# An expert stage's gated products: their transposes and parts one unit of weights sooner, their activation ahead of the context's second products

## The chip, the core and the metric

The kernel runs on one core of one Trainium2 chip. The metric is device time in microseconds (us) of one execution, lower is better. Five engines work side by side, each through its own queue in order: TensorE (PE in the profile, with PEld for the loading of its weights), VectorE (DVE), ScalarE (ACT), GpSimd (POOL) and SyncE (SP, which here only issues loads).

## The reference, cut to what matters

The network has two layers. Each ends in an expert stage: 16 experts of 1024 x 512 gate and up weights and 512 x 1024 down weights, in float32. Each expert takes the `cap` tokens that score highest for it: 128 of the 1024 latent tokens, and in the first layer also 32 of the 256 context tokens.

```python
def expert_choice_ffn(h, w_router, w_gate, w_up, w_down):
    n, dm = h.shape[1], h.shape[2]
    cap = EC_FACTOR * n // N_EXPERTS
    aff = jax.nn.softmax(jnp.einsum('bnd,de->bne', h, w_router).astype(jnp.float32), axis=-1)
    g, idx = lax.top_k(aff.swapaxes(1, 2), cap)
    xs = jax.vmap(lambda hb, ib: hb[ib])(h, idx)
    act = jax.nn.silu(jnp.einsum('becd,edf->becf', xs, w_gate)) * jnp.einsum('becd,edf->becf', xs, w_up)
    ys = jnp.einsum('becf,efd->becd', act, w_down) * g[..., None].astype(h.dtype)
    ...
for l in range(DEPTH):
    need_ctx = l < DEPTH - 1
    ...
    x = x + mod_l[5] * expert_choice_ffn(h, moe_router[l], moe_w_gate[l], moe_w_up[l], moe_w_down[l])
    if need_ctx:
        ...
        ctx = ctx + mod_c[5] * expert_choice_ffn(hc, moe_router[l], moe_w_gate[l], moe_w_up[l], moe_w_down[l])
```

## The kernel before

Almost every operation is recorded at line 162, a helper, so the rows are told apart by tiles: `A` holds the rounded weights and their remainders (and the context's tokens), `C` the raw weights as loaded, `W` the tokens' parts and the results, `M` small tiles, among them the gated products, and `ps` the PSUM banks.

**One unit of weights** is 512 KB: 256 rows of a gate or an up matrix, or 128 rows of a down matrix. An expert has twelve: four pairs of gate and up, four of down. `sources` gives their order of loading, in which expert e-1's down units come between the first and the second half of expert e's gate and up units. `fetch` loads a unit into one of ten `C` buffers, on SP's queue. `issue` splits it: ScalarE copies it rounded into `hi` (`A<-C`, ACTIVATE), VectorE subtracts to `lo` (`A<-C,A`, TENSOR_TENSOR). In layer 1 every sixth subtraction goes to GpSimd instead. Three products, high by high, low by high and high by low, stand for one in full precision.

**One expert** in `experts`, under a manual schedule, in which each engine keeps the order in which the code emits: four calls of `gate_up` (k = 0 to 3, each six 128x512 products of one unit, then the `issue` of a later unit), in layer 0 the context's products with the same four raw units (`ctx`, 64 products `ps<-C,A`, after which the four `C` buffers are free and four loads are issued), then `down` for expert e-1 (four units, 24 products `ps<-A,M`, in layer 0 followed by 32 products `ps<-C,M` of the context), then the next tokens' parts (`parts`), four more `gate_up` calls (k = 4 to 7), `ctx` for these units, and `activate`. In layer 1 (`need` is false) there is no context work, and `issue` itself fetches the next unit.

**Around the change.** `activate` makes the gated product `act`: ScalarE's Silu of the gate's bank (`M<-ps`, 128x512 f32), then VectorE's product with the up bank (`M<-M,ps`); in layer 0 also a 128x128 one for the context. One expert later `turn(e-1)`, called after `gate_up` of k = 1, transposes `act` on TensorE (four `ps<-cf,M`, and in layer 0 a fifth for the context), copies the result rounded to `ah` on ScalarE (`M<-ps`, fp32r) and subtracts to `al` on VectorE (`M<-ps,M`). In layer 0 ScalarE also copies the context's part. `down` needs `ah` for its first two products and `al` from its third on. In three experts (e = 1, 5, 9) `slots` makes the next routing table: VectorE builds tiles after k = 0, TensorE takes them in eight products `ps<-M,M` after k = 3.

The last expert's `turn` and `down` (e = 16) run after the loop's weights are through.

Of the kernel before, what the change touches and what calls it, by code (L numbers as in the profile page):

```python
# [15 lines left out]
AF = mybir.ActivationFunctionType  # L16
# [25 lines left out]
         g=7, v=0.079, hgrn0=6.614, hgrn1=6.757, group0=1.91, group1=3.41, hout0=6.767, hout1=3.44, chunk=6.713, prep=1.5,  # L42
# [123 lines left out]
class Model:  # L166
# [1651 lines left out]
    def experts(self, l, need, base, basec, h2d, h2c):  # L1818
# [4 lines left out]
        nc, a = self.nc, self.a  # L1823
# [4 lines left out]
        X, XT, XC, ACT, AT = {}, {}, {}, {}, {}  # L1828
# [14 lines left out]
        def fetch(gone=0):  # L1843
            nonlocal live
            live -= gone
            while live < raws:
                s = next(src, None)
                if s is None:
                    return
                w = self.t("C", [128, D])  # L1850
                nc.sync.dma_start(w, s)
                raw.append(w)
                live += 1

        def issue(early=False):
            nonlocal unit
            if not raw:
                return
            w = raw.pop(0)
            u = unit % ring  # L1860
            hi, lo = rows[u], rows[ring + u]
            nc.scalar.activation(hi, w, AF.Copy)
            (nc.gpsimd if early or (not need and unit % 6 == 5) else nc.vector).tensor_sub(lo, w, hi.bitcast(F32))
            unit += 1
            ready.append((w, hi, lo))
            if not need:
                fetch(1)

        def prep(e):
            it, vt = self.it[:, e:e + 1], self.vt[:, e:e + 1]  # L1870
            X[e] = (self.gather(h2d, it), it, vt)
# [28 lines left out]
                nc.vector.tensor_sub(xl[:, hs], pt, xh[:, hs].bitcast(F32))  # L1900
            return xh, xl

        def gate_up(e, u, g, p):

            xh, xl = XT[e]
            w, hi, lo = ready.pop(0)
            for k in range(2):
                c = slice(512 * k, 512 * k + 512)
                for pas, (xx, ww) in enumerate(((xh, hi), (xl, hi), (xh, lo))):
                    nc.tensor.matmul(p, xx[:, 2 * u + k], ww[:, c], start=(u == 0 and k == 0 and pas == 0),  # L1910
                                     stop=(u == 3 and k == 1 and pas == 2))
            issue()
            return u, g, w

# [8 lines left out]
                                         stop=(u == 3 and k == 1 and g == 1))  # L1923
                fetch(1)

        def activate(e, pg, pu, pc):
            act = self.t("M", [128, 512])
            nc.scalar.activation(act, pg, AF.Silu)
            nc.vector.tensor_mul(act, act, pu)
            actc = None  # L1930
            if need:
                actc = self.t("M", [128, 128])
                nc.scalar.activation(actc, pc[:, 0:128], AF.Silu)
                nc.vector.tensor_mul(actc, actc, pc[:, 128:256])
            ACT[e] = (act, actc)

        def turn(e):

            act, actc = ACT.pop(e)
            pt = self.p([128, 4, 128])  # L1940
            for i in range(4):
                nc.tensor.transpose(pt[:, i, :], act[:, 128 * i:128 * i + 128], self.ident)
            ah = self.t("M", [128, 4, 128], F32R)
            al = self.t("M", [128, 4, 128], F32R)
            nc.scalar.activation(ah, pt, AF.Copy)
            nc.vector.tensor_sub(al, pt, ah.bitcast(F32))
            ct = None
            if need:
                pt = self.p([128, 4, 128])
                nc.tensor.transpose(pt[:, 0, :], actc, self.ident)  # L1950
                ct = self.t("M", [128, 128])
                nc.scalar.activation(ct, pt[:, 0, :], AF.Copy)
            AT[e] = (ah, al, ct)

        def down(e):
            _, it, vt = X.pop(e)
            ah, al, ct = AT.pop(e)
            py = [self.p() for _ in range(2)]
            units = []
            for f in range(4):  # L1960
                w, hi, lo = ready.pop(0)
                for pas, (xx, ww) in enumerate(((ah, hi), (al, hi), (ah, lo))):
                    for hf in range(2):
                        nc.tensor.matmul(py[hf], xx[:, f], ww[:, 512 * hf:512 * hf + 512],
                                         start=(f == 0 and pas == 0), stop=(f == 3 and pas == 2))
                issue()
                units.append(w)
                yield "s"
            if need:
                pyc = self.p()  # L1970
                for f, w in enumerate(units):
                    for q in range(4):
                        nc.tensor.matmul(pyc[32 * q:32 * q + 32, :256], ct[:, 32 * f:32 * f + 32],
                                         w[:, 256 * q:256 * q + 256], start=f == 0, stop=f == 3)
                    fetch(1)
            ys = self.t("W", [128, D])
            for hf in range(2):
                c = slice(512 * hf, 512 * hf + 512)
                nc.vector.scalar_tensor_tensor(ys[:, c], py[hf], vt, G5[hf], op0=ALU.mult, op1=ALU.mult)
            nc.gpsimd.indirect_dma_start(out=base, out_offset=bass.IndirectOffsetOnAxis(ap=it, axis=0),  # L1980
                                         in_=ys, in_offset=None, compute_op=ALU.add)
            if need:
                yc = self.t("M", [128, 256])
                nc.vector.scalar_tensor_tensor(yc, pyc[:, :256], self.vc[:, e:e + 1], G5c, op0=ALU.mult, op1=ALU.mult)
                nc.gpsimd.indirect_dma_start(out=basec.rearrange("n (q d) -> (n q) d", q=4),
                                             out_offset=bass.IndirectOffsetOnAxis(ap=self.ic4[:, e:e + 1], axis=0),
                                             in_=yc, in_offset=None, compute_op=ALU.add)
# [20 lines left out]
        with self.tc.manual_schedule():  # L2008
            prep(0)
            yield True  # L2010
            prep(1)
            issue()
            yield 3.0
            XT[0] = parts(X[0][0])
            while len(ready) < ahead:
                issue()
            for e in range(17):
                if e < 16:
                    pg, pu = self.p(), self.p()
                    pc = self.p() if need else None  # L2020
                    units = []
                    for k in range(4):
                        units.append(gate_up(e, k // 2, k % 2, (pg, pu)[k % 2]))
                        if k == 1 and e:
                            turn(e - 1)
                        if e % 4 == 1 and e < 12:
                            if k == 0:
                                table = self.slots(e // 4 + 1)
                            if k in (0, 3):
                                next(table)  # L2030
                        if k == 0 and e + 2 < 16:
                            prep(e + 2)
                        yield "s"
                    if need:
                        ctx(e, units, pc)
                        yield "s"
                else:
                    turn(e - 1)
                if e:
                    yield from down(e - 1)  # L2040
                    yield "s"
                if e < 16:
                    if e % 4 == 1 and e < 12:
                        next(table, None)
                    if e + 1 < 16:
                        if need and (e + 1) % 4 == 0:
                            turn_ctx((e + 1) // 4)
                        XT[e + 1] = parts(X[e + 1][0])
                        if need and e % 4 == 1 and e < 12:
                            gather_ctx(e // 4 + 1)  # L2050
                    units = []
                    for k in range(4, 8):
                        units.append(gate_up(e, k // 2, k % 2, (pg, pu)[k % 2]))
                        yield "s"
                    if need:
                        ctx(e, units, pc)
                    activate(e, pg, pu, pc)
                yield "s"

    def layer(self, l):  # L2060
# [83 lines left out]
```

## Time and profile before

| | |
|---|---|
| median of 3 runs | 2811.71 us (2805.24 to 2816.72) |
| the profiled execution's own time | 2805.08 us |
| its span, first to last instruction | 2803.1 us |
| mean granted TensorE clock | 0.925 |
| busy: PE, PEld, DVE, ACT, POOL | 2414.1, 1839.7, 1842.1, 1188.1, 832.9 us |
| expert stage of layer 0, about | 1131 to 1572 us |
| expert stage of layer 1, about | 2486 to 2803 us |

The profiled execution is one of the program, with its own time; the span is 2 us less than that. Times of rows are counted from the start of the span. A timeline row merges like instructions that follow each other; in brackets stands how long the engine was idle just before and what it was waiting for. The ends of matrix products are modelled, so gaps on TensorE are better read from start to start.

### The profile page before, as it was taken

To read this page: it belongs to the slowest core of one execution; us is meant where nothing else is said; L and a number is where in the kernel's file an instruction comes from. 1 tells how busy PE (TensorE), PEld (TensorE's weight loads), DVE (VectorE), ACT (ScalarE), POOL (GpSimd) and SP (SyncE) were. 2 spreads that over 40 slices of the span, in tenths; PEclk is the share of its full clock that TensorE was granted. 3 is DMA by queue.
4 is the path that set the end of the run, shared out by engine and by line. 5 is a ranking of instruction groups with operands and counts; after the bars stand their busy time and mean duration, and the time that the engine had idled before them with its cause. 6 is when DMAs were issued, how large, how long until landed. Compare 5 with 4: busy or idle time off the path is not lost. (4 is left out here: it accounts for less than half of the span.)

```text
span 2803.1 us, 49842 instructions
## 1 busy us (share of the span) xinstructions
PE 2414.1 (86%) x19212; PEld 1839.7 (66%) x19212; DVE 1842.1 (66%) x3638; ACT 1188.1 (42%) x2010; POOL 832.9 (30%) x898
## 2 busy tenths in 40 slices
PE   6879999998898885899999599889968988759997
PEld 3658888654554663677777587779645546547786
DVE  5445477575787546677677746672777865489996
ACT  3345223234335112455565352432352342247774
POOL 3112232241532113121221422421353411324553
PEclk8889999999999887899999799989988999879999
DMA  6221226368313434688888511132331023559997
GB/s 253 64 68 50 72 79 193 124 205 293 110 44 100 145 117 145 213 286 287 282 293 292 158 50 42 55 91 86 111 116 48 27 100 123 192 189 379 384 389 244
DMA packets 243436, 455.40 MB, mean 162 GB/s; under 512 B 25688, under 2 KB 155096, under 8 KB 242176
## 3 DMA queue, kind: packets, MB, share of 16 engines
q1 hardware_dynamic: 190176, 365.75, 37.6%
q0 software_dynamic: 12096, 37.75, 5.7%
q10 hardware_dynamic: 40928, 48.72, 4.9%
q8 instruction: 151, 2.47, 0.4%
q14 instruction: 85, 0.70, 0.1%
HBM read 377.55 MB, written 74.60 MB: 161 GB/s over the span
## 5 line engine op out<-in xcount | busy, mean ns | idle before, releaser
L162 PE MATMUL ps<-A,W 128*128 128x512 f32 (+3 forms) x4160 | 962.2, 378 | 34.4 <-ACT W L162 31.5
L162 PEld LDWEIGHTS ps<-A,W 128*128 128x128 f32 x4160 | 737.4, 194 | 178.9 <-ACT W L162 35.4
L162 DVE TENSOR_TENSOR A<-C,A 128x1024 fp32r<-128x1024 f32 x342 | 420.0, 1257 | 123.6 <-ACT A L162 117.7
L162 ACT ACTIVATE A<-C 128x1024 fp32r<-128x1024 f32 x384 | 398.2, 1059 | 194.3 <-DMA C<-in_moe_w_down_dram 75.8
L162 ACT ACTIVATE M<-ps 128x512 f32<-128x512 f32 (+6 forms) x576 | 262.7, 469 | 487.0 <-PE ps L162 407.2
L162 PE MATMUL ps<-W,A 128*128 128x256 f32 x1344 | 191.2, 298 | 7.2 <-DVE A L162 6.9
L162 PE MATMUL ps<-A,M 128*128 128x512 f32 x768 | 185.2, 394 | 5.7 <-DVE M L162 4.2
L162 PEld LDWEIGHTS ps<-W,A 128*128 128x128 f32 x1344 | 176.1, 202 | 9.9 <-DVE A L162 7.4
L162 PEld LDWEIGHTS ps<-A,M 128*128 128x128 f32 x768 | 141.5, 188 | 42.6 <-DVE M L162 9.5
L162 POOL TENSOR_TENSOR C<-C,M 128x512 f32<-128x512 f32 x76 | 110.6, 1467 | 194.3 <-ACT M L162 133.1
L162 POOL TENSOR_TENSOR A<-C,A 128x1024 fp32r<-128x1024 f32 x42 | 119.3, 2846 | 157.9 <-ACT A L162 127.1
L162 DVE TENSOR_TENSOR C<-C,M 128x512 f32<-128x512 f32 (+2 forms) x196 | 128.9, 670 | 40.7 <-ACT M L162 39.2
L162 PE MATMUL ps<-cf,M 128*128 128x128 f32 (+3 forms) x416 | 71.3, 297 | 96.2 <-DVE M L162 58.8
L162 PE MATMUL ps<-C,A 128*32 128x128 f32 (+1 forms) x2528 | 146.5, 288 | 0.0
L162 PEld LDWEIGHTS ps<-C,A 128*32 128x32 f32 (+1 forms) x2528 | 133.9, 126 | 10.7 <-issue 5.6
L162 PE MATMUL ps<-A 96*128 96x512 f32 (+3 forms) x368 | 132.2, 415 | 9.3 <-ACT A L162 4.0
L162 PE MATMUL ps<-A,C 128*128 128x512 f32 x352 | 134.2, 412 | 1.6 <-DVE C L162 1.4
L162 PEld LDWEIGHTS ps<-cf,M 128*128 128x128 f32 (+2 forms) x416 | 52.5, 150 | 124.2 <-issue 41.3
L162 ACT ACTIVATE W<-ps 128x512 fp32r<-128x512 f32 (+2 forms) x156 | 66.3, 476 | 158.2 <-PE ps L162 157.8
L162 ACT ACTIVATE C<-ps 128x512 f32<-128x512 f32 (+4 forms) x116 | 53.9, 469 | 183.5 <-PE ps L162 171.7
L162 POOL DMA_INDIRECT dr<-W,it x16 | 25.3, 1579 | 335.2 <-DVE W L162 335.2
L162 POOL TENSOR_TENSOR W<-W,C 128x512 f32<-128x512 f32 x33 | 49.7, 1526 | 249.8 <-DVE W L162 163.6
(244 smaller groups left out, 3910.3 us busy)
## 6 DMA issues: line engine op xcount, KB each, us to landing
C<-in_moe_w_gate_dram SPq DMA_DIRECT2D x128, 512.0 KB, 10.9
C<-in_moe_w_up_dram SPq DMA_DIRECT2D x128, 512.0 KB, 5.0
C<-in_moe_w_down_dram SPq DMA_DIRECT2D x128, 512.0 KB, 8.2
W<-in_ada_w_dram SPq DMA_DIRECT2D x80, 512.0 KB, 4.6
W<-in_w_in_dram SPq DMA_DIRECT2D x40, 512.0 KB, 3.7
C<-dr SPq DMA_DIRECT2D x29, 512.0 KB, 3.6
dr<-M ACTq DMA_DIRECT2D x114, 128.0 KB, 2.7
M<-dr SPq DMA_DIRECT2D x46, 256.0 KB, 4.5
```

What stands on the lines that cost most here:

```text
L162: return f(*args, **kw)
```

## The change

The activation of the latents and that of the context become functions of their own. `activate` is called before `ctx` for the second four units, `activate_ctx` after it. `turn` is left with the latents' four transposes and their two parts, and `turn_actc` does the context's transpose. `gate_up` takes a function that it calls between its products and its `issue`. In layer 0 this is `turn` in k = 0 and `turn_actc` in k = 1; in layer 1 it is `turn` in k = 1.

```diff
-        def gate_up(e, u, g, p):
+        def gate_up(e, u, g, p, then=None):
 ...
                                      stop=(u == 3 and k == 1 and pas == 2))
+            if then:
+                then()
             issue()
             return u, g, w
 ...
-        def activate(e, pg, pu, pc):
-            act = self.t("M", [128, 512])
+        def activate(e, pg, pu):
+            act = ACT[e] = self.t("M", [128, 512])
             nc.scalar.activation(act, pg, AF.Silu)
             nc.vector.tensor_mul(act, act, pu)
-            actc = None
-            if need:
-                actc = self.t("M", [128, 128])
-                nc.scalar.activation(actc, pc[:, 0:128], AF.Silu)
-                nc.vector.tensor_mul(actc, actc, pc[:, 128:256])
-            ACT[e] = (act, actc)
+
+        def activate_ctx(e, pc):
+            actc = ACT[e, 1] = self.t("M", [128, 128])
+            nc.scalar.activation(actc, pc[:, 0:128], AF.Silu)
+            nc.vector.tensor_mul(actc, actc, pc[:, 128:256])
 ...
-            AT[e] = (ah, al, ct)
+            AT[e] = (ah, al)
+
+        def turn_actc(e):
+            pt = self.p([128, 4, 128])
+            nc.tensor.transpose(pt[:, 0, :], ACT.pop((e, 1)), self.ident)
+            ct = AT[e, 1] = self.t("M", [128, 128])
+            nc.scalar.activation(ct, pt[:, 0, :], AF.Copy)
 ...
-                        units.append(gate_up(e, k // 2, k % 2, (pg, pu)[k % 2]))
-                        if k == 1 and e:
-                            turn(e - 1)
+                        back = (turn, turn_actc) if need else (None, turn)
+                        then = back[k] if e and k < 2 else None
+                        units.append(gate_up(e, k // 2, k % 2, (pg, pu)[k % 2], then and (lambda: then(e - 1))))
 ...
+                    activate(e, pg, pu)
                     if need:
                         ctx(e, units, pc)
-                    activate(e, pg, pu, pc)
+                        activate_ctx(e, pc)
```

TensorE in layer 0, at expert 4's unit k = 0, whose products go to `ps_16014` and those of k = 1 to `ps_16015` (`M_16007` and after it `M_15967` is `act` of expert 3):

```order
 L162 MATMUL ps_16014<-A_14752,W_15916 128x512
 L162 MATMUL ps_16014<-A_14753,W_15915 128x512
+L162 MATMUL ps_16023<-cf_66,M_15967 128x128 x4
 L162 MATMUL ps_16015<-A_14752,W_15915 128x512
 L162 MATMUL ps_16015<-A_14752,W_15916 128x512
```

The four transposes now stand between the products of k = 0 and those of k = 1. The same engine at the end of k = 1:

```order
 L162 MATMUL ps_16015<-A_14752,W_15916 128x512
 L162 MATMUL ps_16015<-A_14754,W_15915 128x512
-L162 MATMUL ps_16036<-cf_66,M_16007 128x128 x4
-L162 MATMUL ps_16045<-cf_66,M_16010 128x128
+L162 MATMUL ps_16043<-cf_66,M_16010 128x128
 L162 MATMUL ps_16014<-A_14752,W_15915 128x512
 L162 MATMUL ps_16014<-A_14752,W_15916 128x512
```

The context's single transpose stays where it was. ScalarE over the same expert before, from Silu to the copies of units that `issue` emits in k = 0 to 3:

```order
L162 ACTIVATE M_16007<-ps_15737 128x512
L162 ACTIVATE M_16010<-ps_15739 128x128
L162 ACTIVATE A_14752<-C_15975 128x1024
L162 ACTIVATE A_14752<-C_15985 128x1024
L162 ACTIVATE M_16041<-ps_16036 128x512
L162 ACTIVATE M_16047<-ps_16045 128x128
L162 ACTIVATE A_14752<-C_15995 128x1024
```

and after:

```order
L162 ACTIVATE M_15967<-ps_15737 128x512
L162 ACTIVATE M_16010<-ps_15739 128x128
L162 ACTIVATE M_16028<-ps_16023 128x512
L162 ACTIVATE A_14752<-C_15978 128x1024
L162 ACTIVATE M_16045<-ps_16043 128x128
L162 ACTIVATE A_14752<-C_15988 128x1024
L162 ACTIVATE A_14752<-C_15998 128x1024
```

The two Silu rows keep their places. The latents' rounded part (`M_16041`, after it `M_16028`) passes the two unit copies that stood ahead of it, and the context's part passes one. In layer 1 TensorE's and VectorE's orders don't change; on ScalarE, at expert 7:

```order
 L162 ACTIVATE M_32072<-ps_31904 128x512
 L162 ACTIVATE A_30628<-C_31947 128x1024
+L162 ACTIVATE M_32102<-ps_32097 128x512
 L162 ACTIVATE A_30628<-C_31958 128x1024
-L162 ACTIVATE M_32106<-ps_32101 128x512
 L162 ACTIVATE A_30627<-C_31971 128x1024
```

The latents' rounded part now stands ahead of the copy of the unit that k = 1 issues.

## Rows read from the trace of the kernel before

**Rows 1.** the page's first line, whole program
```profile
span 2803.1 us, 49842 instructions
```

**Rows 2.** stretches: us, busy us (x instructions) PE PEld DVE ACT POOL, PEclk, DMA, GB/s
```profile
1150.00:1530.00 380.00, 362.48 (x3632) 282.68 (x3621) 275.63 (x321) 220.99 (x268) 70.82 (x43) 0.99 0.86 284
2500.00:2760.00 260.00, 250.94 (x1202) 205.84 (x1201) 237.75 (x253) 193.53 (x220) 123.62 (x52) 1.00 1.02 380
```

**Rows 3.** waits of PE, 1150 to 1530: us in total, times, longest us
```profile
PE ps L162 <- DVE M L162: 8.9, 14, 1.7
...
PE ps L162 <- ACT M L162: 0.4, 1, 0.4
```

**Rows 4.** PE timeline: start us, us, engine line op out<-in xcount [idle before <-releaser]
```profile
1232.99 3.02 PE L162 MATMUL ps<-A,W 128*128 128x512 f32 x12
1235.84 0.71 PE L162 MATMUL ps<-cf,M 128*128 128x128 f32 x5
1236.31 3.00 PE L162 MATMUL ps<-A,W 128*128 128x512 f32 x12
...
1241.12 0.73 PE L162 MATMUL ps<-A,M 128*128 128x512 f32 x2
1242.47 5.28 PE L162 MATMUL ps<-A,M 128*128 128x512 f32 x22 [0.62 <-DVE M L162]
```

**Rows 5.** ACT timeline of the same stretch
```profile
1230.59 0.58 ACT L162 ACTIVATE M<-ps 128x512 f32<-128x512 f32 x1
...
1237.17 1.06 ACT L162 ACTIVATE A<-C 128x1024 fp32r<-128x1024 f32 x1 [3.77 <-DMA C<-in_moe_w_down_dram]
1239.50 1.06 ACT L162 ACTIVATE A<-C 128x1024 fp32r<-128x1024 f32 x1 [1.27 <-DVE A L162]
1240.47 0.75 ACT L162 ACTIVATE M<-ps 128x512 fp32r<-128x512 f32 x2
```

**Rows 6.** DVE timeline of the same stretch
```profile
1232.57 0.68 DVE L162 TENSOR_TENSOR M<-M,ps 128x512 f32<-128x512 f32 x1
...
1241.74 0.68 DVE L162 TENSOR_TENSOR M<-ps,M 128x512 fp32r<-128x512 f32 x1
```

**Rows 7.** PE timeline, a down block without a break
```profile
1270.37 5.73 PE L162 MATMUL ps<-A,M 128*128 128x512 f32 x24
```

**Rows 8.** PE timeline, first and last of eight broken down blocks, layer 0
```profile
1190.83 5.28 PE L162 MATMUL ps<-A,M 128*128 128x512 f32 x22 [0.71 <-DVE M L162]
...
1480.92 5.27 PE L162 MATMUL ps<-A,M 128*128 128x512 f32 x22 [0.65 <-DVE M L162]
```

**Rows 9.** PE timeline, gate blocks before two late products
```profile
1151.07 3.01 PE L162 MATMUL ps<-A,W 128*128 128x512 f32 x12
...
1313.01 3.02 PE L162 MATMUL ps<-A,W 128*128 128x512 f32 x12
```

**Rows 10.** DVE timeline, those two late products
```profile
1153.24 0.89 DVE L162 TENSOR_TENSOR M<-M,ps 128x512 f32<-128x512 f32 x2 [0.69 <-ACT M L162]
...
1314.59 0.88 DVE L162 TENSOR_TENSOR M<-M,ps 128x512 f32<-128x512 f32 x2
```

**Rows 11.** PE timeline, a wait for the routing table's tiles
```profile
1266.12 0.32 PE L162 MATMUL ps<-M,M 128*128 128x80 bf16 x4 [1.73 <-DVE M L162]
```

**Rows 12.** ACT timeline, the rounded copy ahead of that wait
```profile
1261.87 1.06 ACT L162 ACTIVATE A<-C 128x1024 fp32r<-128x1024 f32 x1 [3.39 <-DMA C<-in_moe_w_down_dram]
```

**Rows 13.** ACT timeline, layer 1, one expert
```profile
2614.87 2.17 ACT L162 ACTIVATE A<-C 128x1024 fp32r<-128x1024 f32 x2
2618.74 0.60 ACT L162 ACTIVATE M<-ps 128x512 fp32r<-128x512 f32 x1 [1.70 <-PE ps L162]
```

**Rows 14.** gate weights' loads, whole program, issue to landing
```profile
DMA to landing us min/median/max: 3.6/10.9/12.8
```

**Rows 15.** two stretches after waits, columns as in group 2
```profile
1266.50:1270.00 3.50, 3.28 (x60) 2.91 (x64) 3.50 (x5) 1.69 (x2) 0.00 (x0) 0.51 0.23 49
1373.00:1377.00 4.00, 3.78 (x75) 3.25 (x76) 4.00 (x5) 1.94 (x2) 0.00 (x0) 1.00 0.46 140
```

More of the change, by code (lines that the diff above doesn't have):

```diff
@@ L1924, in ctx @@
                 fetch(1)
-        def activate(e, pg, pu, pc):
-            act = self.t("M", [128, 512])
+        def activate(e, pg, pu):
+            act = ACT[e] = self.t("M", [128, 512])
             nc.scalar.activation(act, pg, AF.Silu)
             nc.vector.tensor_mul(act, act, pu)
-            actc = None
-            if need:
-                actc = self.t("M", [128, 128])
-                nc.scalar.activation(actc, pc[:, 0:128], AF.Silu)
-                nc.vector.tensor_mul(actc, actc, pc[:, 128:256])
-            ACT[e] = (act, actc)
+        def activate_ctx(e, pc):
+            actc = ACT[e, 1] = self.t("M", [128, 128])
+            nc.scalar.activation(actc, pc[:, 0:128], AF.Silu)
+            nc.vector.tensor_mul(actc, actc, pc[:, 128:256])
         def turn(e):
-            act, actc = ACT.pop(e)
+            act = ACT.pop(e)
             pt = self.p([128, 4, 128])
@@ L1946, in turn @@
             nc.vector.tensor_sub(al, pt, ah.bitcast(F32))
[L1947 to L1952, printed above, removed]
-            AT[e] = (ah, al, ct)
+            AT[e] = (ah, al)
[4 more added lines that the diff above has]
+            nc.scalar.activation(ct, pt[:, 0, :], AF.Copy)
         def down(e):
             _, it, vt = X.pop(e)
-            ah, al, ct = AT.pop(e)
+            ah, al = AT.pop(e)
             py = [self.p() for _ in range(2)]
@@ L1970, in down @@
                 pyc = self.p()
+                ct = AT.pop((e, 1))
                 for f, w in enumerate(units):
@@ L2038, in experts @@
                     turn(e - 1)
+                    if need:
+                        turn_actc(e - 1)
                 if e:
```

## The prediction

> **What bounds the kernel now.** I read the page first, then stretches of the two expert stages, then the waits of TensorE, then single experts. The change touches nothing outside the two stages, so what counts is which engine or queue sets the pace in each. The rest of the 2803.1 us span [rows 1] can only slide.
>
> In layer 0 it is TensorE: in 380 us it is busy for 362.5, at a granted clock of 0.99, while the DMA share is 0.86 [rows 2]. Its idle time behind VectorE's small tiles is 8.9 us in 14 waits, plus one of 0.4 behind ScalarE [rows 3]. Six of the 14 stand before the routing table's products in experts 1, 5 and 9 (one of them, 1.73, is in [rows 11]; all six 4.7 us together); the other eight stand inside `down`'s block (the first and the last of them in [rows 8]).
>
> In layer 1 the DMA share is 1.02 at 380 GB/s [rows 2], and a load takes up to 12.8 us to land where the least is 3.6 [rows 14]: the queue is full, and the stage ends when the weights have come. TensorE is busy there too (250.9 of 260 us), but what it loses is given back to a stream of loads that doesn't wait for it.
>
> **How the wait in layer 0 arises.** Take the expert in [rows 4 to 6]. The transposes start at 1235.84, the twelve products after them at 1236.31, so `ah` could start some 0.1 us after that. It starts at 1240.47, because two copies of weight units stand ahead of it in ScalarE's queue, and those wait for their loads: 1237.17 (3.77 us idle, behind a down load) and 1239.50 [rows 5]. So `al` comes at 1241.74 and ends at 1242.42 [rows 6]. TensorE starts `down` at 1241.12, does two products with `ah`, and stops for `al` until 1242.47 [rows 4]. The block then ends at 1242.47 + 5.28 = 1247.75, 6.63 us after its start, where an unbroken one takes 5.73 [rows 7]: 0.90 lost. (The gap itself reads 0.62, since ends of products are modelled.) Subtracted in this way, nine of fifteen blocks lose between 0.3 and 1.0 us, 6.7 in sum; with the 0.4 us in which one block waited for `ah` itself [rows 3] it is **7.1 us** that late parts cost.
>
> **The change, part by part.**
>
> *Activation ahead of the context's second products.* Zero. It is moved past TensorE's 64 products and SP's loads, but each engine keeps its own order, and on ScalarE and VectorE nothing stood between: the Silu rows stay in place in the order shown, and in the trace Silu already starts at 1230.59 [rows 5], before the gate block's twelve products of the next expert at 1232.99 [rows 4] and so beside the context's products between them. No DMA of another queue is passed that waits for it. This half doesn't do what its words say.
>
> *Transposes one unit sooner, layer 0.* They start some 1.43 us (half of 1235.84 - 1232.99) earlier on TensorE, and, what is more, `ah` passes both unit copies. `ah` then ends about 0.7 us after the transposes, `al` 0.8 us later (0.68 us [rows 6] and a handover), so `al` is there within 2 us, while TensorE has 18 products and the context's 64 before `down`, some 6.3 us (1241.12 - 1236.31 = 4.8, and 1.43 more). The late parts' 7.1 us go whole, with some 4 us of cover left. What is late next: the table's tiles, below.
>
> *The new wait.* The transposes need `act`, VectorE's product, 1.43 us sooner. Mostly it is ready: in the expert above it ends at 1232.57 + 0.68 = 1233.25 [rows 6], 1.2 us before 1234.42. But VectorE is sometimes behind with its subtractions. With the half block at 1151.07 + 1.43 = 1152.50 [rows 9] and the product over at 1153.24 + 0.68 = 1153.92 [rows 10], TensorE will stand for 1.4 us; at 1313.01 + 1.43 = 1314.44 against 1315.27, for 0.8. By the same subtraction over all fifteen, four more are late: 0.7, 0.5, 0.1 and 0. The 0.5 falls in expert 5, where it costs nothing: TensorE waits 1.73 us later in that expert for table tiles [rows 11], which stand on VectorE behind a subtraction whose copy waits 3.39 us for its load [rows 12], and neither moves. In expert 1 that copy does not wait for a load; it now stands behind `ah`, and the table's tiles slide by the same 1.4 us, which I count once. Queued behind the waiting transposes on TensorE is the rest of the expert, and behind `ah` on ScalarE the copy for k = 0, used five units later. Sum **+3.0 us**.
>
> *Splitting five transposes into four and one.* Five take 0.47 us from start to start [rows 4]; a single one by itself is not in this stage. Bounds: nothing, or one share of it more (0.09) in each of fifteen experts, 1.4 us. I take half, **+0.7**.
>
> *Layer 1.* TensorE's and VectorE's orders stand; on ScalarE the copy for k = 1 goes behind `ah`. At 2614.87 two copies ran in one go, the second from about 2615.9, and `ah` at 2618.74 [rows 13], so the copy moves to about 2619.3, 3.4 us later. GpSimd subtracts from it and then frees a raw buffer, for which one of SP's loads waits, with the loads behind it. Cover: the loads take around 11 us (median 10.9) to land against 3.6 for one that waits for no other [rows 14], so some 7 us of queue stand ahead. The price is 0 while the cover holds. A gain I exclude: `ah` already comes right after the transposes there, 1.70 us after ScalarE had nothing else to do [rows 13], and what it passes was done by then.
>
> **Sum:** -7.1 + 3.0 + 0.7 = -3.4 us, all in layer 0. That makes 2805.08 - 3.4 = 2801.7 us for an execution like the profiled one. That execution lies 0.2 us below the lowest of the three runs shown, and 6.6 us below their median of 2811.71. In terms of the median: 2811.7 - 3.4 = **2808 us**, -0.1%.
>
> **Rivals.**
>
> 1. *The wait only changes its name.* VectorE is late because the loads are, and these are issued when TensorE's context products free buffers; a faster `down` leaves VectorE less time, and products that now just make it (the 0.1 and 0 above) come late too. If six more of the fifteen are late by 0.5 us each, 3 us of the gain are gone: 2811 us. For it: in half of the experts the subtractions run back to back into the product. Against it: the loads that decide are issued after `down`, hence after the wait that goes. 0.15.
>
> 2. *The clock, slower than before.* After the wait of 1.73 us [rows 11] the granted clock reads 0.51 for 3.5 us (the first row of [rows 15]), the lower level of 1.2 GHz against 2.4; after another of 1.69 us it read 1.00 (the second row there). Each such stretch costs 1.7 us. If the three longest new waits (1.4, 0.8, 0.7) each bring one, 5.2 us are added: -3.4 + 5.2 = +1.8, 2813 us. It decides from the second stretch on. Against it: the stage's 0.99 [rows 2] is 3.8 us lost to the clock, two or three such stretches among some twenty waits, so most waits bring none. 0.10. The Trainium skill speaks for this rival: TensorE: Matmul & The Clock Gate, "A second HAM failure mode: psum-queue depth-cycling", says that short idles between groups of products, often enough, make the clock swing between its levels. By that rule the change would trade nine idles for five and the sum would be anything between -3.4 and this +1.8; the trace agrees in one of the two waits of 1.7 us.
>
> 3. *Layer 1 starves.* If the cover of 7 us is gone, the 3.4 us by which the copy moves come through in each of up to fourteen experts: +48 us, 2856 us; with half of it, 2832. For it: SP's loads queue in order, so one late buffer holds the next ones. Against it: [rows 14]. 0.05.
>
> 4. *Faster by more.* If the waits that go also take away the stretch at the lower clock in layer 0 (1.7 us) and layer 1 gave back the 9.1 us in which TensorE isn't busy [rows 2], the sum would be -3.4 - 1.7 - 9.1 = -14.2: 2798 us. For that the loads would have to speed up, against the share of 1.02. 0.05. The Trainium skill would leave room for it: Perfetto Trace Analysis, "Roofline", puts the practical ceiling of one core at about 435 GB/s, above the 380 measured; the measured share of the engines says full.
>
> **How the numbers follow.** My forecast: 0.65, 2808 us. The model's own ends are -7 (no late product, no price for the split) and +2 (rival 2). The three runs shown spread from 2805 to 2817, 6 us to each side, which is more than the effect. With both the range is 2797 to 2818 us, which holds the forecast and rivals 1 and 2, and most of rival 4. A measurement of this kernel can tell about 0.5%, 14 us, from no change. Faster by over that needs rival 4 and luck: 0.06. Slower by over it needs rival 3: 0.06. Within it: 0.88.
>
> **What the profile after would show.** In layer 0 no row of `down` with a gap behind VectorE, all blocks at 5.7 us; `ah` right after four transposes, before the copy for k = 0. New gaps before the transposes of a third of the experts, 1.4 us in expert 1 and 0.1 to 0.8 in the others; the waits for table tiles of experts 5 and 9 still there. The stage of layer 0 shorter by 2 to 5 us, that of layer 1 as long as before with the DMA share at 1.0. Wrong would be: a layer 1 with gaps in the loads or TensorE waiting for copies; a layer 0 whose new waits exceed 5 us; or a granted clock below 0.97 between 1150 and 1530.

## Result, and the profile after

The changed kernel takes **2839.4 us** (median of 4 runs, 2836.1 to 2842.0) against 2810.5 for the kernel before (4 runs beside it): ratio 1.0102, 95% interval 1.0079 to 1.0124. The forecast was 2808 us and no measurable change; it is 1.0% slower, by 29 us.

The two stretches of [rows 2], in the profile after (same columns: TensorE, its weight loads, VectorE, ScalarE, GpSimd, granted clock, DMA share, GB/s):

```profile
1150.00:1530.00 380.00, 360.95 (x3585) 281.69 (x3583) 276.78 (x319) 220.56 (x265) 71.11 (x43) 0.98 0.86 283
2500.00:2760.00 260.00, 236.40 (x1100) 192.56 (x1098) 241.82 (x234) 172.38 (x203) 106.15 (x50) 0.97 0.99 349
```

Layer 0 reads almost as before. In layer 1 TensorE gets through 1100 instructions in the 260 us where it got through 1202, yet VectorE is busier: 241.8 us for 234 instructions, 1.03 us each, where it was 237.75 for 253, 0.94 each.

**Layer 0.** The late parts at `down` are gone, as forecast. Its group on the page, with the idle time ahead of it in the last column, showed 5.7 us before, 4.2 of them behind VectorE (first row); now it shows 0.9, and that behind ScalarE (second row). The eight gaps of [rows 8] are gone:

```profile
L162 PE MATMUL ps<-A,M 128*128 128x512 f32 x768 | 185.2, 394 | 5.7 <-DVE M L162 4.2
L162 PE MATMUL ps<-A,M 128*128 128x512 f32 x768 | 184.3, 396 | 0.9 <-ACT M L162 0.9
```

TensorE's timeline in expert 1 shows the new wait ahead of the four transposes (third row; 1.4 us was forecast; 1.09 is the gap, and by starts it is 1154.91 - 1152.17 = 2.74 where 1.49 is usual, so 1.25), the fifth transpose by itself (fifth row), and the two short waits for table tiles behind it:

```profile
1150.28 1.95 PE L162 MATMUL ps<-C,A 128*32 128x128 f32 x64
1152.17 1.65 PE L162 MATMUL ps<-A,W 128*128 128x512 f32 x6
1154.91 0.66 PE L162 MATMUL ps<-cf,M 128*128 128x128 f32 x4 [1.09 <-DVE M L162]
1155.32 1.64 PE L162 MATMUL ps<-A,W 128*128 128x512 f32 x6
1156.79 0.27 PE L162 MATMUL ps<-cf,M 128*128 128x128 f32 x1
1156.82 2.98 PE L162 MATMUL ps<-A,W 128*128 128x512 f32 x12
1160.33 0.32 PE L162 MATMUL ps<-M,M 128*128 128x80 bf16 x4 [0.53 <-DVE M L162]
```

**Layer 1** is where the time went. GpSimd's scatters into the output come once in an expert: in the trace of before the first of eleven stands at 2554.97 and the last at 2744.59, 18.96 us apart on average; after, ten of them run from 2567.92 to 2755.68. First before, then after:

```profile
2554.97 2.46 POOL L162 DMA_INDIRECT out_dram<-W,it  x1 [0.16 <-DVE W L162]
...
2744.59 2.46 POOL L162 DMA_INDIRECT out_dram<-W,it  x1 [0.16 <-DVE W L162]
```
```profile
2567.92 1.59 POOL L162 DMA_INDIRECT out_dram<-W,it  x1 [2.69 <-DVE W L162]
...
2755.68 1.60 POOL L162 DMA_INDIRECT out_dram<-W,it  x1 [2.68 <-DVE W L162]
```

That is 20.86 us for an expert, 1.90 more, and with 15 such experts 28.5 us: the whole loss.

What ScalarE waits for in layer 1 after (2500 to 2760; us in total, times, longest), the complete answer:

```profile
ACT M L162 <- PE ps L162: 52.2, 12, 5.8
ACT W L162 <- PE ps L162: 26.8, 13, 2.9
ACT A L162 <- PE ps L162: 5.7, 7, 1.6
```

It waits for no load any more. In the same view of before these rows stood among others:

```profile
ACT A L162 <- DMA C<-in_moe_w_gate_dram: 17.9, 18, 2.2
ACT A L162 <- DMA C<-in_moe_w_up_dram: 14.9, 22, 1.4
```

So the weights are early now, and somebody later in the chain is slow.

### The profile page after: what moved, and what is told of

It reads as the page before. It is cut to its first block, busy times and chain, and to the rows that moved or that the text cites. A ratio compares the mean times of both kernels' runs of the same rounds, so it can differ in the third digit from the quotient of the medians.

```text
span 2838.7 us, 49853 instructions
## 1 busy us (share of the span) xinstructions
PE 2425.4 (85%) x19212; PEld 1849.9 (65%) x19212; DVE 1879.6 (66%) x3638; ACT 1183.7 (42%) x2010; POOL 821.6 (29%) x898
## 5 line engine op out<-in xcount | busy, mean ns | idle before, releaser
L162 DVE TENSOR_TENSOR A<-C,A 128x1024 fp32r<-128x1024 f32 x342 | 455.3, 1364 | 95.1 <-ACT A L162 89.9
L162 ACT ACTIVATE A<-C 128x1024 fp32r<-128x1024 f32 x384 | 391.4, 1057 | 124.2 <-PE ps L162 36.6
L162 PE MATMUL ps<-cf,M 128*128 128x128 f32 (+3 forms) x416 | 78.1, 310 | 117.5 <-DVE M L162 80.7
L162 PE MATMUL ps<-cf,W 128*128 128x128 f32 (+1 forms) x536 | 87.6, 304 | 44.6 <-POOL W L162 22.4
```

Source lines behind the costliest of these rows:

```text
L162: return f(*args, **kw)
```

## What VectorE and GpSimd do beside each other

Both form low parts of weight units, `A<-C,A`: the raw weights minus their rounded copy, both in SBUF. GpSimd takes one unit in six. In an expert of layer 1 these are the unit behind the second products (called k1 here) and the one behind the fourth product group of `down` (d3).

One expert of **before**, VectorE and then GpSimd (start us, duration, count, idle ahead of it):

```profile
2704.04 1.40 DVE L162 SCALAR_TENSOR_TENSOR W<-ps,vt,M 128x512 f32<-128x512 f32 x2
2705.36 1.28 DVE L162 TENSOR_TENSOR W<-ps,W 128x512 fp32r<-128x512 f32 x2
...
2711.69 1.22 DVE L162 TENSOR_TENSOR A<-C,A 128x1024 fp32r<-128x1024 f32 x1
2713.16 0.69 DVE L162 TENSOR_TENSOR M<-ps,M 128x512 fp32r<-128x512 f32 x1 [0.25 <-ACT M L162]
2714.11 3.31 DVE L162 TENSOR_TENSOR A<-C,A 128x1024 fp32r<-128x1024 f32 x2 [0.25 <-ACT A L162]
```
```profile
2704.21 2.42 POOL L162 TENSOR_TENSOR A<-C,A 128x1024 fp32r<-128x1024 f32 x1 [7.96 <-ACT A L162]
...
2711.82 3.37 POOL L162 TENSOR_TENSOR A<-C,A 128x1024 fp32r<-128x1024 f32 x1 [0.93 <-ACT A L162]
```

GpSimd's d3 subtraction (2704.21) lies beside four VectorE instructions that have one tensor input in PSUM and one in SBUF (`W<-ps,...`; `vt` is a factor for each row). None of them is longer than elsewhere: two in 1.40, two in 1.28. Its k1 subtraction (2711.82 to 2715.19) starts 0.13 us behind a VectorE subtraction (2711.69) and takes 3.37 us instead of 2.42. It lies beside `al`, which has an input in PSUM and keeps its 0.69, and runs 1.1 us into VectorE's next subtractions: the two from 2714.11 take 3.31 us, where two alone take 2.35 (below), so 0.96 is lost.

The same of **after**:

```profile
2701.83 0.69 DVE L162 TENSOR_TENSOR M<-ps,M 128x512 fp32r<-128x512 f32 x1 [0.24 <-ACT M L162]
2703.72 9.36 DVE L162 TENSOR_TENSOR A<-C,A 128x1024 fp32r<-128x1024 f32 x5 [1.20 <-ACT A L162]
2713.00 1.40 DVE L162 SCALAR_TENSOR_TENSOR W<-ps,vt,M 128x512 f32<-128x512 f32 x2
```
```profile
2702.82 2.41 POOL L162 TENSOR_TENSOR A<-C,A 128x1024 fp32r<-128x1024 f32 x1 [5.53 <-ACT A L162]
2708.50 3.49 POOL L162 TENSOR_TENSOR A<-C,A 128x1024 fp32r<-128x1024 f32 x1 [3.27 <-ACT A L162]
```

ScalarE now makes `ah` first and then the copy that GpSimd's k1 unit needs, and only then one for VectorE. Three things follow. VectorE stands 1.20 us for its next copy, where it stood 0.25. GpSimd starts 1.0 us after `al` starts, where it started 1.3 us before it, so it lies right ahead of VectorE's run of subtractions, not beside `al`. And d3 (2708.50) now falls into that run, 4.5 us ahead of the `W<-ps,...` instructions, since it follows ScalarE, and VectorE has fallen behind ScalarE. The run holds five subtractions. Pieces of it, read in narrow windows:

```profile
2703.72 2.60 DVE L162 TENSOR_TENSOR A<-C,A 128x1024 fp32r<-128x1024 f32 x1 [1.20 <-ACT A L162]
2706.24 2.35 DVE L162 TENSOR_TENSOR A<-C,A 128x1024 fp32r<-128x1024 f32 x2
2708.51 4.56 DVE L162 TENSOR_TENSOR A<-C,A 128x1024 fp32r<-128x1024 f32 x2
```

The first takes 2.60 us, the next two 2.35 together, the last two 4.56. GpSimd's first ends at 2702.82 + 2.41 = 2705.23, VectorE's first at 2706.32, that is 1.09 later, about the time of one alone. GpSimd's second starts while the third of the run still has 0.09 us to go, and takes 3.49 instead of 2.41, 1.08 longer, about the time of the fourth; then the fifth of the run waits until GpSimd is through (2711.99) and ends at 2713.07. So the two never work side by side here: whichever comes second waits for the end of the other's instruction.

The Trainium skill says this in SBUF — State Buffer, "Who interferes with whom": a VectorE instruction with two SBUF inputs contends with a GpSimd instruction that reads SBUF; the one that starts first keeps the shared ports for the whole instruction, and one with a single SBUF input isn't touched. The trace agrees in both halves: 2.60 and 3.49 us against 1.22 and 2.41 alone, and the `W<-ps,...` rows of before at their usual length.

**Theories.** *One:* the k1 copy, late by `ah`, sets VectorE back; GpSimd's two subtractions then both block VectorE's, and VectorE becomes the pace. *Two* (the forecast's third rival): the raw buffer comes free late and loads land late. *Three:* ScalarE's new order by itself keeps VectorE waiting, whatever GpSimd does. The waits above already speak against two.

## Experiments

| kernel | median us | ratio to before, 95% interval |
|---|---|---|
| changed kernel | 2839.4 | 1.0102 (1.0079 to 1.0124) |
| l0_only | 2809.8 | 0.9985 (0.9972 to 0.9997) |
| l1_only | 2837.3 | 1.0090 (1.0071 to 1.0109) |
| after_nopool | 2801.6 | 0.9963 (0.9947 to 0.9979) |
| before_nopool | 2808.1 | 0.9988 (0.9974 to 1.0002) |
| before_hold | 2818.9 | 1.0040 (1.0015 to 1.0065) |
| after_beside | 2839.9 | 1.0120 (1.0095 to 1.0145) |
| after_k1vec | 2804.8 | 0.9978 (0.9956 to 1.0001) |
| after_d3vec | 2810.4 | 1.0010 (0.9993 to 1.0026) |
| after_next | 2827.2 | 1.0057 (1.0036 to 1.0078) |
| l0_nopool | 2804.0 | 0.9973 (0.9955 to 0.9990) |
| after_nopool_b | 2803.7 | 0.9969 (0.9954 to 0.9984) |

The kernel before had medians of 2812.0 to 2812.3 us beside these runs.

**Which layer.** l0_only, on the changed kernel:

```diff
-                        then = back[k] if e and k < 2 else None
+                        then = back[k] if need and e and k < 2 else None
                         units.append(gate_up(e, k // 2, k % 2, (pg, pu)[k % 2], then and (lambda: then(e - 1))))
+                        if not need and e and k == 1:
+                            turn(e - 1)
```

> The changed kernel with layer 1 put back as before: there the transposes of the activation stand behind the issue of the unit that follows the second products, so that ScalarE copies that unit ahead of `ah`. Layer 0 keeps the change. If the whole loss is layer 1's (all theories below), the time is within 0.3% of the kernel before, 2805 to 2815 us; the working ahead of the result gives 2807 (3.4 us saved), the trace of the changed kernel's layer 0 stage gives about 1 us lost, 2811. If layer 0 has a part in the loss that its own stage does not show (clock, load order carried over), it is above 2820.

Measured 0.9985: 4.2 us gained, between 0.8 and 7.9. The forecast's sum of 3.4 lies in that interval, and so does 1 us (the medians differ by 2.2). The traces show no gain: from the stage's first gate product to the last product of `down` it is 418.3 us before, 419.5 after and 419.6 in l0_only. Over the four traces here with the old layer 0 it is 415.4 to 421.2, 418.3 on average; over the nine with the new one 417.2 to 420.7, 418.8 on average. So the run allows a small gain in layer 0, and the traces show none.

l1_only, on the kernel before (`gate_up` calls `then` ahead of `issue()`, as in the change):

```diff
-                        units.append(gate_up(e, k // 2, k % 2, (pg, pu)[k % 2]))
-                        if k == 1 and e:
+                        early = not need and k == 1 and e
+                        units.append(gate_up(e, k // 2, k % 2, (pg, pu)[k % 2], (lambda: turn(e - 1)) if early else None))
+                        if need and k == 1 and e:
                             turn(e - 1)
```

> The kernel before with one edit alone: in layer 1 the transposes of the activation and `ah`, `al` go ahead of the issue of the unit behind the second products. If layer 1's order alone is the cause, 2835 to 2842 us, as the changed kernel; if it needs layer 0's part too, under 2820.

Measured 1.0090, 25 us lost: layer 1's order alone makes the loss.

**GpSimd away.** after_nopool and before_nopool carry the same line:

```diff
-            (nc.gpsimd if early or (not need and unit % 6 == 5) else nc.vector).tensor_sub(lo, w, hi.bitcast(F32))
+            (nc.gpsimd if early else nc.vector).tensor_sub(lo, w, hi.bitcast(F32))
```

> The changed kernel, but in layer 1 VectorE makes every low part, the one in six that GpSimd made among them. VectorE then has 2 more subtractions of 1.2 us in each expert, with nothing of GpSimd's beside them. Theory 1 (GpSimd's subtraction, three us later, runs beside VectorE's subtractions and both are stretched; VectorE becomes the pace): the order of ScalarE no longer matters, so the time is that of the same edit on the kernel before, within 6 us; by VectorE's sum (16.9 us busy in 18.5 us of an expert, plus 2.4 us) some 2815 to 2840. Theory 2 (the raw buffer comes free late and loads land late) and theory 3 (ScalarE's later copies by themselves keep VectorE waiting): it stays 15 to 30 us above the same edit on the kernel before.

> The kernel before, but in layer 1 VectorE makes every low part. Theory 1: the same time as the changed kernel with this edit, within 6 us, 2815 to 2840 us. Theories 2 and 3: 15 to 30 us under it.

Measured 2801.6 and 2808.1 us. With GpSimd's subtractions gone the order that cost 25 us costs nothing; the changed kernel is even the faster of the two by its ratio, though the intervals touch, and from what is not shown. So theory three falls as the whole cause: ScalarE's order is the same in the changed kernel and in after_nopool. The amount came out better than my 2815 to 2840, which had added two subtractions to a VectorE sum that I took for the pace. Stretch 2560 to 2740 of the changed kernel and of after_nopool, columns as above, and the group of subtractions in it (busy us, mean ns, idle ahead):

```profile
2560.00:2740.00 180.00, 163.40 (x752) 133.13 (x750) 168.17 (x162) 116.96 (x138) 74.78 (x35) 0.96 1.00 352
```
```profile
L162 DVE TENSOR_TENSOR A<-C,A 128x1024 fp32r<-128x1024 f32 x88 | 128.1, 1508 | 7.3 <-ACT A L162 7.2
```

And of after_nopool:

```profile
2560.00:2740.00 180.00, 174.78 (x831) 142.20 (x830) 173.93 (x194) 131.53 (x152) 38.26 (x19) 1.00 1.03 386
```
```profile
L162 DVE TENSOR_TENSOR A<-C,A 128x1024 fp32r<-128x1024 f32 x116 | 135.4, 1220 | 4.0 <-ACT A L162 3.8
```

Ten subtractions of an expert beside GpSimd's two take VectorE 10 x 1.508 = 15.1 us; all twelve without GpSimd take 12 x 1.220 = 14.6. In the new order GpSimd's help cost VectorE more than the work that it took over. In the order of before it did not: ten took 10 x 1.285 = 12.9 us there. The same two rows of before:

```profile
2560.00:2740.00 180.00, 173.41 (x830) 142.12 (x829) 162.03 (x172) 132.31 (x151) 86.91 (x37) 1.00 1.03 385
```
```profile
L162 DVE TENSOR_TENSOR A<-C,A 128x1024 fp32r<-128x1024 f32 x95 | 118.6, 1285 | 13.8 <-ACT A L162 13.4
```

**The blocking by itself.** after_beside is after_nopool with a GpSimd subtraction for the same units whose result nobody reads:

```diff
+        Z = self.t("Z", [128, 832])
...
+            if not need and unit % 6 == 5:
+                nc.gpsimd.tensor_sub(Z, hi[:, 0:832].bitcast(F32), hi[:, 0:832].bitcast(F32))
```

> The changed kernel with all low parts of layer 1 on VectorE (2801.6 us), and beside them, for one unit in six, a GpSimd subtraction whose result nobody reads: it takes the unit's high part twice and writes 832 of 1024 columns of a tile of its own, and neither PE, VectorE nor a load waits for it. Theory 1a (GpSimd and VectorE stretch one another in SBUF, whatever the data): VectorE's subtractions beside it take 2.4 us and more in place of 1.22, and with VectorE at 97% busy the time goes to 2825 to 2870 us. Theory 1b (PE waits for the low part that GpSimd delivers late): 2800 to 2806 us, as without it.

Measured 1.0120: 38 us come back on top of after_nopool, though no raw buffer, no low part and no load hangs on GpSimd. So neither late loads (theory two) nor late low parts (theory 1b) are needed for the loss; and since ScalarE waits for no load in the changed kernel, theory two falls. All of VectorE's subtractions in the same stretch (duration ns min/median/max), here and then in after_nopool:

```profile
L162 DVE TENSOR_TENSOR A<-C,A x102: 1202/1211/2598, 2559.0 to 2739.4; 128x1024 fp32r<-128x1024 f32 x102
```
```profile
L162 DVE TENSOR_TENSOR A<-C,A x116: 1212/1219/1227, 2559.8 to 2739.3; 128x1024 fp32r<-128x1024 f32 x116
```

The median is the same; what differs is the longest, 2598 ns against 1227: a few subtractions that wait, not a general slowing.

**Which of the two.** after_k1vec leaves GpSimd only d3, after_d3vec only k1:

```diff
-            (nc.gpsimd if early or (not need and unit % 6 == 5) else nc.vector).tensor_sub(lo, w, hi.bitcast(F32))
+            (nc.gpsimd if early or (not need and unit % 12 == 11) else nc.vector).tensor_sub(lo, w, hi.bitcast(F32))
```

(after_d3vec has `unit % 12 == 5`.)

> The changed kernel; in layer 1 GpSimd keeps only the unit of the fourth `down` block, the one behind the second products goes to VectorE. Theory 1, with the second products' unit as the place: the loss goes, 2800 to 2815 us. If GpSimd's other subtraction takes as much: 2820 to 2830 us.

> The changed kernel; in layer 1 GpSimd keeps only the unit behind the second products, the one of the fourth `down` block goes to VectorE. Theory 1, with the second products' unit as the place: most of the loss stays, 2818 to 2842 us. If the other subtraction makes the loss: 2800 to 2812 us.

Measured 0.9978 and 1.0010. I had expected the loss in one of them; it is in neither, so it takes both. In after_k1vec d3 has moved back beside `W<-ps,...` and blocks next to nothing (mean VectorE subtraction 1222 ns, longest 1605):

```profile
2704.11 2.42 POOL L162 TENSOR_TENSOR A<-C,A 128x1024 fp32r<-128x1024 f32 x1 [12.65 <-ACT A L162]
```
```profile
2703.92 1.40 DVE L162 SCALAR_TENSOR_TENSOR W<-ps,vt,M 128x512 f32<-128x512 f32 x2
2705.24 1.28 DVE L162 TENSOR_TENSOR W<-ps,W 128x512 fp32r<-128x512 f32 x2
```

In after_d3vec the 1.20 us of waiting and one blocked subtraction of 2.61 us are there in most experts, as in the changed kernel, and the time is that of before within 0.3%. The k1 copy alone sets VectorE back by little more than VectorE can spare; what makes the loss is that d3 then falls among subtractions too.

**GpSimd late, ScalarE as before.** before_hold keeps the old orders of ScalarE and VectorE and holds GpSimd's k1 subtraction until `ah` is there:

```diff
-            issue()
+            issue(hold=hold)
...
+                        if hold:
+                            lo, w, hi = hold[0]
+                            nc.gpsimd.tensor_copy(self.t("s1", [128, 1]), AT[e - 1][0][:, 0, 0:1].bitcast(F32))
+                            nc.gpsimd.tensor_sub(lo, w, hi.bitcast(F32))
+                            fetch(1)
```

> The kernel before; in layer 1 GpSimd's subtraction of the unit issued behind the second products is held until `ah` is there (a tiny GpSimd copy of one column of `ah` stands ahead of it), and the load that takes its raw buffer is asked for behind it. ScalarE's and VectorE's orders stay those of before. Theory 1 (it is GpSimd's subtraction some 3 us later that makes the loss): 2828 to 2842 us. Theory 3 (ScalarE's order makes it): 2808 to 2816 us. The run that took GpSimd out of the changed kernel already speaks against theory 3.

Measured 1.0040, 11 us, between 4 and 18: below what theory one said, above what three said. Blocking is as large as in the changed kernel (1503 ns mean here in the stretch of 2560 to 2740), but VectorE waits for copies only 1.8 us there instead of 7.2. That points to a share of ScalarE's order of its own.

**The next unit for GpSimd.** after_next lets VectorE have ScalarE's first copy behind `ah`:

```diff
-            (nc.gpsimd if early or (not need and unit % 6 == 5) else nc.vector).tensor_sub(lo, w, hi.bitcast(F32))
+            (nc.gpsimd if early or (not need and unit % 12 in (6, 11)) else nc.vector).tensor_sub(lo, w, hi.bitcast(F32))
```

> The changed kernel; in layer 1 GpSimd takes the unit after the one behind the second products (and still that of the fourth `down` block), so that ScalarE's first copy behind `ah` is one for VectorE. It tells two parts of the loss apart. Part a, the stretching by two GpSimd subtractions in an expert, stays; part b, VectorE standing 1.2 us in each expert since ScalarE first copies a unit for GpSimd, goes (0.24 us is left). If part b is about two thirds of the loss, as the run with GpSimd's subtraction held suggests (7 us lost of 28): 2815 to 2825 us. If the gap is worth nothing: 2832 to 2842 us.

Measured 1.0057, 16 us, between the two answers: the waits shrank only from 7.2 to 6.5 us in the stretch and blocking grew (1595 ns mean). So neither this run nor before_hold takes waiting and blocking apart, and how the 25 us divide between them stays open.

**What layer 1's new order is worth without GpSimd.** l0_nopool is l0_only with the line of after_nopool; after_nopool_b is after_nopool again, beside it.

> Layer 0 with the change, layer 1 in the order of before, all of layer 1's low parts on VectorE. Beside the same with layer 1 in the new order (next run) it gives what the new order of layer 1 is worth by itself, with GpSimd out of the way: if it gains, this one is 2 to 5 us slower than the next; if it is worth nothing, the two are within 2 us, at 2800 to 2806 us.

> The changed kernel with all low parts of layer 1 on VectorE once more, in more rounds, beside the run before: 2801.6 us by its first run, 0.4% under the kernel before. If that stands, it is faster than the kernel before and the changed kernel.

Measured 2804.0 and 2803.7: nothing either way. The changed kernel with GpSimd out of layer 1 is 0.3 to 0.4% faster than the kernel before in both measurements, and with l0_nopool the fastest here. What makes that is not shown. The ratios of l0_only (0.15%) and before_nopool (0.12%) would add up to it, but the interval of before_nopool reaches to no change, and the traces show no shorter stage of layer 0.

**The account.** An expert's length (mean distance of the scatters), and VectorE's busy time of the stretch 2560 to 2740 scaled to one expert (after: 168.17 x 20.86 / 180 = 19.5; the others likewise):

| kernel | expert us | VectorE busy in it |
|---|---|---|
| after_nopool | 18.8 | 18.2 |
| before | 19.0 | 17.1 |
| after_k1vec | 19.1 | 17.3 |
| after_d3vec | 19.7 | 18.6 |
| before_hold | 20.2 | 19.3 |
| after_next | 20.5 | 19.6 |
| after | 20.9 | 19.5 |
| after_beside | 21.3 | 20.9 |

TensorE is busy 18.3 us of an expert (after_nopool: 174.78 x 18.80 / 180). Up to about that VectorE's sum doesn't show in the time. Above it an expert gets longer with VectorE's sum, and it is TensorE that waits for VectorE: in the same stretch 6.5 us before, 16.6 after (the rows below), 5.0 in after_nopool and 21.7 in after_beside.

```profile
PE ps L162 <- DVE M L162: 6.5, 7, 1.8
```
```profile
PE ps L162 <- DVE M L162: 16.6, 9, 2.3
```
(The spans of the profiled executions of after_d3vec, 2822 us, and of before_hold, 2821, lie above the medians of these kernels, so their rows overstate what they cost.)

## Why the prediction was wrong, point by point

- **The failing step** is the part on layer 1: "The price is 0 while the cover holds." It priced the moved copy only by the raw buffer and the loads behind it. The cover held: ScalarE waits for no load after. The instruction that hangs on the moved copy, GpSimd's subtraction, I followed only to the buffer that it frees, and not to the engine beside which it would now run. Missing was a term of 1.9 us in each of 15 experts.
- **"TensorE's and VectorE's orders stand"** was true and didn't help: the same ten subtractions in the same order took 1508 ns instead of 1285 each.
- **The bound of layer 1** was misread. [Rows 2] have VectorE at 237.75 of 260 us, 91%; I took the DMA share of 1.02 for the limit and passed over VectorE. After, that share is still 0.99 while the bytes fell from 380 to 349 GB/s: it doesn't tell whether the queue is the limit.
- **Rival 3** gave 2832 to 2856 us, near the measured time, but by late loads, for which there is no row. The price was right by accident; the chance of 0.05 was the chance of another mechanism.
- **Layer 0**: the late parts went, but a second term failed, the one for the new waits, and the sum of -3.4 is not shown. Term by term:
  - *Late parts*, forecast -7.1. Summed from the first product of each `down` block to its last, the blocks lose 7.2 us against unbroken ones before, 0.4 after and 0.7 in l0_only.
  - *New waits*, forecast 3.0 in five places that count. By starts, as the forecast reckoned, and with 1.49 us for six products that wait for nothing, they come to 5.4 us after (4.2 by the gaps) and 4.5 in l0_only. In expert 3 it is 1.9 (0.7 was forecast; 0.3 in l0_only), behind the gate block of 1313.01 only 0.2 (0.8 was forecast), and 0.4 to 0.6 in experts 11, 13, 14 and 15, for which at most 0.1 was forecast.
  - *The split*, forecast 0.7. A gate block with its five transposes takes 3.35 us where nothing waits, against 3.32 before: 0.5 in fifteen experts.
  - With these the sum is about -1. The interval of l0_only (-7.9 to -0.8) holds that and -3.4 alike; l0_nopool's ratio lies 0.15% under before_nopool's, but their intervals overlap. The traces of the stage show nothing gained. The activation half, priced at nothing, was not tried by itself.
- **Rival 1** (the wait changes its name) holds by the traces. All of TensorE's waits between 1150 and 1530 are 17.4 us before, 19.0 after and 17.9 in l0_only. The rows of before that [rows 3] leaves out, then all rows of after:

```profile
PE ps L162 <- DVE W L162: 6.9, 3, 2.6
PE ps L162 <- ACT A L162: 1.2, 3, 0.6
```
```profile
PE ps L162 <- DVE M L162: 8.6, 12, 2.0
PE ps L162 <- DVE W L162: 8.1, 3, 3.1
PE ps L162 <- ACT A L162: 2.3, 3, 1.6
```

- **Rival 2** (clock) has a small share in layer 0 at most: 0.98 against 0.99. In layer 1 the clock fell from 1.00 to 0.97 as TensorE began to wait; after_next has 0.99 in the stretch 2560 to 2740 and still 20.5 us an expert, so the clock follows the loss rather than makes it.
- **The range**: 7 us below and 2 above 2811.7, with 6 to each side for the spread, are 2799 to 2820 us, not 2797 to 2818. The measured 2839.4 lies outside both.

## To carry to other kernels

When a change moves an operation, follow it to the instruction that consumes it on every engine, and ask not only what that one frees but what it will now run beside: VectorE and GpSimd on SBUF operands take turns. An engine at 91% beside one at 97% is a second bound with a small margin; sum both by stage before calling a delay free. Give the helper engine its share where the busy engine reads PSUM, or not at all: with the new order here twelve subtractions alone were cheaper than ten beside two, with the old order ten beside two were the cheaper.

## What the runs showed of the hardware

A GpSimd subtraction of 128x1024 takes 2.41 us, VectorE's 1.22. The one that comes second waits for the other's end: VectorE's then ends 1.08 to 1.09 us after GpSimd's, and GpSimd's own took 3.49 us when it started 0.09 us before the end of one VectorE subtraction with the next right behind it. VectorE instructions with one input in PSUM keep their length beside the same GpSimd instruction (1.40 and 1.28 us for two). The Trainium skill, GPSIMD Engine Reference, "Key points", puts VectorE at about twice GpSimd's speed for elementwise work; here it is 2.41 / 1.22 = 1.98. What I had not expected is the feedback: a VectorE that has stood 1.2 us for a copy and lost 1.4 us to GpSimd's first instruction meets the next one at a worse place and loses another 2.2 us (4.56 against 2.35).
